# Two RMS norms by products with ones, other pieces of the first weights, and another order of the sample's values in a hybrid decoder step

## The chip, the cores and the metric

The kernel runs on one core of one Trainium2 chip. The time is the device time of one execution in microseconds (us), as a median over several runs. The engines are named as in the profile: PE is the matrix engine (TensorE), DVE the vector engine, ACT the scalar engine, POOL is GpSimd, SP issues most of the DMAs. Each engine works through its own written list of instructions strictly in order and waits for others only by semaphores.

## The reference

One step of one decoder layer, in fp32, for a prompt of 512 positions and 8 sample tokens, so that 520 columns share all weights. In short:

```python
h = rmsnorm(x, norm_mix_g)
q, k, v, u, xq, gates = split_cols(h @ w_in)
o_a = sliding_window_attention(q, k, v)            # 8 heads of 64, 2 kv heads, window 128, blocks of 128
o_b = s5_branch(u)                                 # scan, gelu, two products (glu)
mk, mv = split(rmsnorm(mem, norm_mem_g) @ w_mem_kv)
o_c = memory_attention(xq, mk, mv)                 # 4 heads of 128, 256 memory tokens
g = sigmoid(gates)
x += (g_A * (o_a @ w_br_attn) + g_B * o_b + g_C * (o_c @ w_br_mem)) @ w_out
x += (gelu(causal_conv3(rmsnorm(x) @ w_gate)) * (rmsnorm(x) @ w_up)) @ w_down
y = rmsnorm(x, norm_final_g)
```

The 8 sample tokens bring their own caches: the memory keys and values of the sample (`sk0` to `sk7`, `sv0` to `sv7` below) are read in units like weights.

## The kernel before

**Products.** x stands transposed, 1024 features in 8 blocks of 128 rows (`KB` = 8, "k blocks"), 520 columns in two halves of 260. Every fp32 number is split into a high part (fp32r) and the rest, and each product is made of three (`mm3`): high by high, high by rest, rest by high. A weight unit is 128 columns of a weight matrix, as 128 by 1024 numbers (512 KB). SP loads it into one of two raw buffers (`w_load`, tile `wraw`), ACT copies out the high part (`whi`), DVE subtracts to get the rest (`wlo`), and PE then runs 8 k blocks by 2 halves by 3 products, 48 matmuls. The units of the memory (`mv0` to `mk3`, over 256 tokens) take 24.

**Order.** Units run as written in `SEQ0` and `SEQ` (lines 51 and 53): first k and v together (the "kv" stage, `for k in range(KB)`, line 757), q0 to q3, then `u`, `mv`, `mk`, `xq`, then gates and the branch projections (`gA0 sk0 ...`, `PA`, `sv`, `gC`, `PC`), then glu, the output projection and the channel sub-layer, which the change leaves alone but for the last norm.

**Lanes.** The work beside the units (attention, norms, the S5 scan) is written as generators, "lanes", that yield between steps. While a kernel is written out, a planner (`Clock`, `pump`, `drain`) keeps an estimated clock for each engine and takes, between two products, the first lane that it holds to be ready. The schedule is manual: the order it arrives at is fixed in every engine's list, and the chip follows it whatever the real times are. `drain(lanes)` writes the lanes named to their end, with no products between.

**Sliding-window attention** (`swa`, line 879; 8 calls, two lanes of them running side by side) is a chain through three engines: 4 score products (PE), 4 maxima over scores and biases (DVE), negation, 4 exponentials (ACT), reciprocal and scaling (two heads on DVE, two on ACT), 8 transposes (PE), copies out of PSUM (DVE and ACT), products with v (PE), and the split of the result (ACT, then DVE). All calls must be through before `merged` is allotted: `drain(list(swa_lanes))` in line 1373, which stands between the units xq3 and gA0.

**The two norms.** The mixer norm sums x*x on DVE into `acc`; within q0, `rstd_cols` (line 570) sums over the partitions by 6 products of 88 columns by one, computes the reciprocal root by an integer guess and three Newton rounds on 88 by 6 numbers (11 small DVE instructions and one of 88 by 528), and `rstd_rows` spreads it over 128 rows by 6 products of 88 by 88 and ACT copies. `Q_COL` and `Q_ROW` say behind which blocks of q0 the two stand. The memory's norm (`mem_prep`, line 804) does the same for 256 tokens. k, v and q are multiplied by rstd when they are evacuated; from `u` on the units use a normalised x, which the lane `x_norm` (line 836) makes.

All instructions go through one wrapper in line 259, so that the profile shows L259 for nearly all of them; tiles are told apart by their names: `B` large buffers, `T` (T2) temporaries, `SD` PSUM of the lanes, `mm` PSUM of the units, `TN` tiny tiles.

## Time and profile before

| what | value |
|---|---|
| median of 3 runs | 869.65 us (869.54 to 870.18) |
| the profiled execution | 870.38 us, its span 868.6 us, mean granted clock 0.997 |
| PE busy | 851.2 us, 98% of the span |
| DVE, ACT, POOL busy | 599.8, 409.0, 135.7 us |
| bytes moved by DMA | 110.41 MB, 127 GB/s over the span |

The span is what the profile covers, from the first to the last instruction; 1.8 us of the profiled execution lie outside it. Busy time is the union of an engine's instructions. A timeline row may hold several records of one kind (x8), and a matmul in fp32 leaves two records. Matmuls are pipelined: one of 260 columns lasts 0.28 us in its record, but in a row of them one starts every 0.12 us. Idle time before an instruction is shown in brackets with what ended it.

### The profile page before, as it was taken

The page shows a single profiled execution, that of the slowest core. Times are in us where ns is not written, and L with a number is a line of the kernel's source. Part 1 is how long each engine was busy: PE and PEld are TensorE (multiplying, and loading weights), DVE is VectorE, ACT ScalarE, POOL GpSimd, SP SyncE. Part 2 cuts the span into 40 slices and gives each one's busy share as a digit, 9 for nine tenths or more (in the row PEclk, how much of TensorE's full clock was granted, in tenths as well). Part 3 has the DMA queues.
Part 4 walks back from the last instruction along what each step waited for, and adds up shares of the span by engine and source line. Part 5 has one row for each costly group of instructions (what it writes and reads, how often), then busy time and mean ns, then how long its engine had stood idle before and what let it go on. Part 6 is the DMA issues. An engine that isn't in the chain of part 4 may idle for free.

```text
span 868.6 us, 17715 instructions
## 1 busy us (share of the span) xinstructions
PE 851.2 (98%) x7067; PEld 823.0 (95%) x7067; DVE 599.8 (69%) x1101; ACT 409.0 (47%) x800; POOL 135.7 (16%) x370
## 2 busy tenths in 40 slices
PE   8999999999999999999999999999999999999996
PEld 8998899999789899989999999999999999999995
DVE  6786787985447698213765568787777877777756
ACT  7366565544434322223334434444645545464555
POOL 7888030000000000000000010111112110110100
PEclk9999999999999999999999999999999999999998
DMA  7534482253714523624333323557565655653222
GB/s 264 178 78 122 125 196 80 74 154 116 150 49 146 170 74 97 148 69 184 106 101 97 98 73 100 144 155 185 152 160 151 165 130 153 161 150 83 71 74 98
DMA packets 54737, 110.41 MB, mean 127 GB/s; under 512 B 13968, under 2 KB 25664, under 8 KB 54384
## 3 DMA queue, kind: packets, MB, share of 16 engines
q1 hardware_dynamic: 50816, 97.40, 38.0%
q0 software_dynamic: 3408, 11.27, 6.8%
q8 instruction: 55, 0.90, 0.4%
q10 hardware_dynamic: 432, 0.63, 0.2%
q14 instruction: 26, 0.21, 0.1%
HBM read 104.05 MB, written 6.26 MB: 127 GB/s over the span
## 4 chain that ended last, share of the span: by engine, by line
PE 74%; DVE 11%; issue 9%; ACT 3%; DMA 2%; SPq 0%; POOL 0%; DVEq 0%; ACTq 0%; POOLq 0%
PE mm L259 55%; PE SD L259 19%; DVE T L259 5%; DVE B L259 3%; DVE wlo L259 2%; DMA wraw<-in_w 2%; ACT T L259 1%; ACT whi L259 1%; ACT B L259 1%; DVE TN L259 1%; SPq L259 0%; POOL T L259 0%; DVE M L259 0%; DVEq L2334 0%; DVE it L259 0%
## 5 line engine op out<-in xcount | busy, mean ns | idle before, releaser
L259 PE MATMUL mm<-B,whi 128*128 128x260 f32 (+1 forms) x3632 | 666.5, 284 | 3.5 <-DVE B L259 1.4
L259 PEld LDWEIGHTS mm<-B,whi 128*128 128x128 f32 x3632 | 560.3, 188 | 11.9 <-issue 5.0
L259 PE MATMUL mm<-B,wlo 128*128 128x260 f32 (+1 forms) x1816 | 512.8, 282 | 1.9 <-DVE wlo L259 1.9
L259 PEld LDWEIGHTS mm<-B,wlo 128*128 128x128 f32 x1816 | 342.2, 188 | 2.8 <-DVE wlo L259 2.8
L259 DVE TENSOR_TENSOR wlo<-wraw,whi 128x1024 fp32r<-128x1024 f32 (+1 forms) x149 | 152.4, 1029 | 89.2 <-ACT whi L259 86.2
L259 ACT ACTIVATE whi<-wraw 128x1024 fp32r<-128x1024 f32 (+1 forms) x149 | 132.5, 897 | 73.0 <-PE mm L259 32.6
L259 PE MATMUL SD<-B,whi 128*128 128x260 f32 x464 | 85.9, 282 | 0.0
L259 PEld LDWEIGHTS SD<-B,whi 128*128 128x128 f32 x464 | 71.6, 188 | 0.1
L259 ACT ACTIVATE T<-mm 128x260 f32<-128x260 f32 (+3 forms) x76 | 32.5, 449 | 78.1 <-PE mm L259 78.0
L259 PE MATMUL SD<-B,wlo 128*128 128x260 f32 x232 | 65.6, 283 | 0.0
L259 ACT ACTIVATE B<-T 128x520 fp32r<-128x520 f32 (+2 forms) x48 | 29.7, 618 | 55.5 <-DVE T L259 55.4
L259 ACT ACTIVATE whi<-M 128x512 fp32r<-128x512 f32 x64 | 39.1, 624 | 26.3 <-DVE M L259 19.4
L259 DVE TENSOR_TENSOR wlo<-M,whi 128x512 fp32r<-128x512 f32 x64 | 42.8, 686 | 11.9 <-ACT whi L259 11.8
L259 DVE TENSOR_TENSOR B<-B 128x256 f32<-128x256 f32 (+11 forms) x78 | 36.3, 474 | 15.9 <-ACT B L259 14.4
L259 PEld LDWEIGHTS SD<-B,wlo 128*128 128x128 f32 x232 | 43.6, 188 | 0.0
L259 DVE TENSOR_TENSOR B<-mm,B 128x520 f32<-128x520 f32 (+2 forms) x36 | 22.4, 622 | 27.4 <-PE mm L259 26.8
L259 ACT ACTIVATE B<-SD 128x256 fp32r<-128x256 f32 (+5 forms) x44 | 17.9, 429 | 44.3 <-PE SD L259 44.3
L259 DVE TENSOR_TENSOR B<-SD,B 128x256 fp32r<-128x256 f32 (+6 forms) x43 | 16.5, 396 | 30.3 <-PE SD L259 22.7
L259 PE MATMUL SD<-B 128*64 128x72 f32 (+9 forms) x412 | 37.3, 282 | 0.0
L259 DVE SCALAR_TENSOR_TENSOR T<-T,sm,T 128x512 f32<-128x512 f32 x44 | 33.1, 753 | 2.7 <-ACT T L259 2.2
L259 DVE TENSOR_TENSOR B<-T,B 128x520 fp32r<-128x520 f32 (+2 forms) x50 | 31.2, 637 | 3.7 <-ACT B L259 3.4
L259 PEld LDWEIGHTS SD<-B 128*64 128x64 f32 (+4 forms) x412 | 25.6, 146 | 8.3 <-issue 4.0
(161 smaller groups left out, 801.8 us busy)
## 6 DMA issues: line engine op xcount, KB each, us to landing
wraw<-in_w SPq DMA_DIRECT2D x96, 512.0 KB, 3.6
M<-in_w SPq DMA_DIRECT2D x48, 256.0 KB, 3.6
wraw<-in_w SPq DMA_DIRECT2D x36, 256.0 KB, 3.3
T<-in_w SPq DMA_DIRECT2D x36, 192.0 KB, 4.4
M<-in_w POOLq DMA_DIRECT2D x8, 512.0 KB, 6.6
wraw<-in_w POOLq DMA_DIRECT2D x8, 512.0 KB, 6.3
sv<-in_w SPq DMA_DIRECT2D x12, 192.0 KB, 5.5
B<-in_xT SPq DMA_DIRECT2D x1, 2080.0 KB
```

The lines of the kernel that those rows point to most:

```text
L259: return g(*a, **k)
```

## The change

It has five parts. (1) Both norms sum over the partitions by products of a 128 by 128 matrix of ones with the sums of squares, so that every partition gets the sum; ACT then takes Ln and Exp for a first value and one Newton round of three DVE instructions runs on the full width. The table set for Ln and Exp is loaded at the start. (2) The first two weight units come in pieces of 1, 3 and 4 k blocks instead of two halves, and the loads of x stand between them. (3) Behind the mixer norm, `ahead` moves behind the evacuation of k and v, with the next weight split and one load in its old place. (4) In `SEQ` each `sv` unit moves behind a later unit, and PC0 to PC3 stand otherwise between the last gates. (5) In the last norm the square of the first value is taken by ACT instead of DVE.

```diff
-SEQ = 'gA0 sk0 gA1 sk1 gA2 sk2 gA3 sk3 gA4 sk4 gA5 sk5 gA6 sk6 gA7 sk7 PA0 PA1 sv0 PA2 sv1 PA3 sv2 gC0 sv3 gC1 sv4 gC2 sv5 sv6 gC3 sv7 gC4 PC0 gC5 PC1 gC6 gC7 PC2 PC3'
+SEQ = 'gA0 sk0 gA1 sk1 gA2 sk2 gA3 sk3 gA4 sk4 gA5 sk5 gA6 sk6 gA7 sk7 PA0 PA1 PA2 sv0 PA3 sv1 gC0 sv2 gC1 sv3 gC2 sv4 gC3 sv5 gC4 sv6 sv7 gC5 PC0 PC1 gC6 PC2 gC7 PC3'
...
-    act.activation(warm, ones[:, 0:1], AF.Exp)
+
+    nc.scalar.preload_act_table_set("natural_log_exp_and_others")
+    act.activation(warm, ones[:, 0:1], AF.Ln)
...
+    CUTS = (0, 1, 4, 8)
+    l0, l1 = w_load(0, CUTS), w_load(1, CUTS)
     next(l0)
     next(l1)
-    for k in (1, 2, 3):
-        x_load(k, 1)
+    x_load(0, 1)
+    x_load(1, 1)
+    next(l0)
+    next(l1)
+    x_load(2, 1)
+    x_load(3, 1)
     next(l0)
     next(l1)
...
+    def rstd_sums(part, out, n=NH, halves=(0, 1)):
+        pr = [SD() for _ in halves]
+        for p, h in zip(pr, halves):
+            pe.matmul(p[:, :n], ones, part[:, h * n:(h + 1) * n], start=True, stop=True)
+        for p, h in zip(pr, halves):
+            act.activation(out[:, h * n:(h + 1) * n], p[:, :n], AF.Ln, bias=eps, scale=1.0 / DM)
+        o = out[:, 0:len(halves) * n]
+        act.activation(o, o, AF.Exp, scale=-0.5)
+        v = T2(len(halves) * n)
+        for p, h in zip(pr, halves):
+            act.activation(v[:, h * n:(h + 1) * n], p[:, :n], AF.Identity, bias=eps, scale=1.0 / DM)
+            free(p)
+        return v, o
+
+    def newton(v, o):
+        t = T2(o.shape[1])
+        dve.tensor_tensor(t, o, o, op=OP.mult)
+        dve.scalar_tensor_tensor(t, t, -0.5, v, op0=OP.mult, op1=OP.mult)
+        dve.scalar_tensor_tensor(o, t, 1.5, o, op0=OP.add, op1=OP.mult)
+        free(t, v)
...
     for k in range(KB):
+        if k == 0:
+            for i in (ik, ik + 1):
+                w_split(i, 0, 1)
         split_norm(xraw, C_GMIX, xgh, xgl, k)
-        if k in (0, 2):
-            w_split(ik, k // 2)
-            w_split(ik + 1, k // 2)
-        if k:
+        if k in (1, 3):
+            for i in (ik, ik + 1):
+                w_split(i, CUTS[(k + 1) // 2], CUTS[(k + 3) // 2])
+        if k and k != 3:
             square(k - 1)
+        if k == 4:
+            square(2)
...
             if (h, k) == Q_COL:
-                dcol = rstd_cols([acc], (0, 1), NH)
-                ahead(iq)
-            if (h, k) == Q_ROW:
-                rstd_rows(dcol, rstd)
+                newton(*rstd_sums(acc, rstd))
+                w_split(iq + 1)
+                load(iq + 3)
...
     evac_kv(psv, vT, vs)
+    ahead(iq)
...
-        d = rstd_cols([macc], (0,), 256)
+        v, o = rstd_sums(macc, mrstd, 256, (0,))
         free(macc)
-        yield
-        rstd_rows(d, mrstd, 256, (0,))
-        free(d)
+        yield "dve", 1
+        newton(v, o)
         yield
...
             act.activation(self.v, self.pr, AF.Identity, bias=eps, scale=1.0 / DM)
+            self.t = T2(self.n)
+            act.activation(self.t, self.y, AF.Square)
 
         def newton(self):
-            t = T2(self.n)
-            dve.tensor_tensor(t, self.y, self.y, op=OP.mult)
+            t = self.t
```

Left out are the new signatures of `w_load` and `w_split`, which take k blocks to cut at.

The planner's lists change with it, from the start up to glu0. Three places follow; numbers behind a name tell one buffer from another.

PE of the kernel before, from the last products of unit mv0 (`mm_1222`): scores of one block of the sliding-window attention (`SD_1290`, `SD_1291`) and products with v of another (`SD_1308`).

```order
L259 MATMUL mm_1222<-B_593,whi_1039 128x256 x2
L259 MATMUL mm_1222<-B_593,wlo_1040 128x256
L259 MATMUL SD_1290<-B_123,B_594 128x256 [waits PE_49]
L259 MATMUL SD_1291<-B_123,B_594 128x256 [waits Activation_49]
L259 MATMUL SD_1290<-B_123,B_594 128x256
L259 MATMUL SD_1291<-B_123,B_594 128x256
L259 MATMUL SD_1308<-T2_1251,B_123 64x256 [waits DVE_49]
L259 MATMUL SD_1308<-T2_1252,B_123 64x256
L259 MATMUL SD_1308<-T2_1251,B_123 64x256
L259 MATMUL SD_1308<-T2_1252,B_123 64x256
```

PE of the changed kernel at the same place, between the units mv0 (`mm_1218`) and mv1 (`mm_1250`).

```order
L259 MATMUL mm_1218<-B_579,wlo_1011 128x256
L259 MATMUL mm_1218<-B_579,whi_1010 128x256 x2
L259 MATMUL mm_1218<-B_579,wlo_1011 128x256
L259 MATMUL mm_1250<-B_579,whi_1101 128x256 [waits PE_49,Activation_49]
L259 MATMUL mm_1250<-B_579,whi_1101 128x256
L259 MATMUL mm_1250<-B_579,wlo_1102 128x256
```

Unit mv1 follows at once. From mv0 to mk1 the changed kernel has six memory units with nothing between their products, and the attention's steps stand later.

PE of the kernel before at the seam between xq3 (`mm_2070`) and gA0 (`mm_2149`).

```order
L259 MATMUL mm_2070<-B_597,whi_1879 128x260
L259 MATMUL mm_2070<-B_598,whi_1879 128x260
L259 MATMUL mm_2070<-B_597,wlo_1880 128x260
L259 MATMUL mm_2149<-B_597,whi_1953 128x260 [waits Activation_49]
L259 MATMUL mm_2149<-B_598,whi_1953 128x260
```

PE of the changed kernel at the same seam, from the last product of xq3 (`mm_1859`) on. `SD_1995`, `SD_1996` are transposes of one attention block, called X below, `SD_2022` its products with v; `SD_2028`, `SD_2029` are transposes of a second, Y.

```order
L259 MATMUL mm_1859<-B_583,wlo_1709 128x260
L259 MATMUL SD_1995<-cs_123,T2_1773 128x128 [waits DVE_49,Activation_49]
L259 MATMUL SD_1995<-cs_123,T2_1773 128x128 x3
L259 MATMUL SD_1996<-cs_123,T2_1774 128x128 [waits DVE_49]
L259 MATMUL SD_1996<-cs_123,T2_1774 128x128 x3
L259 MATMUL SD_2011<-cs_123,B_126 8x128 [waits DVE_49]
L259 MATMUL SD_2011<-cs_123,B_126 8x128
L259 MATMUL SD_2022<-T2_2005,B_126 64x256 [waits DVE_49]
L259 MATMUL SD_2022<-T2_2006,B_126 64x256 [waits Activation_49]
L259 MATMUL SD_2022<-T2_2005,B_126 64x256
L259 MATMUL SD_2022<-T2_2006,B_126 64x256
L259 MATMUL SD_2028<-cs_123,T2_1904 128x128 [waits DVE_49,PE_49]
```

PE of the changed kernel, further on in the same seam: the scores of a third block, Z, the last of the eight (`SD_2043`, `SD_2044`), Y's products with v (`SD_2061`), and Z's transposes (`SD_2082`, `SD_2083`).

```order
L259 MATMUL SD_2043<-B_126,B_580 128x256 [waits PE_49]
L259 MATMUL SD_2044<-B_126,B_580 128x256 [waits DVE_49]
L259 MATMUL SD_2043<-B_126,B_580 128x256
L259 MATMUL SD_2044<-B_126,B_580 128x256
L259 MATMUL SD_2061<-T2_2038,B_126 64x256 [waits Activation_49]
L259 MATMUL SD_2061<-T2_2039,B_126 64x256
L259 MATMUL SD_2061<-T2_2038,B_126 64x256
L259 MATMUL SD_2061<-T2_2039,B_126 64x256
L259 MATMUL SD_2082<-cs_123,T2_2052 128x128 [waits DVE_49,Activation_49]
L259 MATMUL SD_2082<-cs_123,T2_2052 128x128 [waits Activation_49]
L259 MATMUL SD_2082<-cs_123,T2_2052 128x128 x2
L259 MATMUL SD_2083<-cs_123,T2_2053 128x128 [waits Activation_49] x2
```

Behind these stand Z's products with v (`SD_2099`), and then gA0. So 32 rows of attention lie between xq3's last and gA0's first product, where the kernel before has none.

ACT of the kernel before around the evacuation of xq3 (`M_1726<-mm_2070`).

```order
L259 ACTIVATE M_1726<-mm_1932 128x520 [waits PE_49]
L259 ACTIVATE whi_2083<-wraw_1957 128x1024 [waits DMAHW4_49]
L259 ACTIVATE M_1726<-mm_2070 128x520 [waits PE_49]
L259 ACTIVATE B_2135<-T2_2136 128x512 [waits DMASW2_49,Pool_49]
L259 ACTIVATE B_2135<-M_1726 128x16 [waits Activation_49]
L259 ACTIVATE B_2135<-T2_2136 128x512
```

ACT of the changed kernel from the evacuation of xq3 (`M_1504<-mm_1859`) on: the exponentials of Y (`T2_1904`, `T2_1905`), the copy of X's transposes (`T2_2006`), the scaling and copy of Y, the exponentials of Z (`T2_2052`).

```order
L259 ACTIVATE M_1504<-mm_1859 128x520 [waits PE_49]
L259 ACTIVATE T2_1904,TN_1903<-T2_1904,TN_1902 128x257 x2
L259 ACTIVATE T2_1905,TN_1903<-T2_1905,TN_1902 128x257 x2
L259 ACTIVATE T2_2006<-SD_1996 128x512 [waits PE_49]
L259 ACTIVATE T2_2014<-SD_2011 8x256 [waits PE_49]
L259 ACTIVATE T2_1905<-T2_1905,TN_1903 128x256 [waits DVE_49]
L259 ACTIVATE T2_1905<-T2_1905,TN_1903 128x256 [waits Activation_49]
L259 ACTIVATE B_793<-SD_2022 128x2x128 [waits PE_49]
L259 ACTIVATE T2_2039<-SD_2029 128x512 [waits PE_49]
L259 ACTIVATE B_793<-SD_2061 128x2x128 [waits PE_49]
L259 ACTIVATE T2_2052,TN_2051<-T2_2052,TN_2050 128x257 [waits DVE_49]
```

In the kernel before no step of the attention follows xq3's evacuation; in the changed one Y's exponentials and all of Z's stand behind it.

## Rows read from the trace of the kernel before

**Rows 1.** The page, busy time and share of the span of each engine
```profile
PE 851.2 (98%) x7067; PEld 823.0 (95%) x7067; DVE 599.8 (69%) x1101; ACT 409.0 (47%) x800; POOL 135.7 (16%) x370
```

**Rows 2.** The page, chain that ended last, shares by engine
```profile
PE 74%; DVE 11%; issue 9%; ACT 3%; DMA 2%; SPq 0%; POOL 0%; DVEq 0%; ACTq 0%; POOLq 0%
```

**Rows 3.** PE's timeline: start us, duration us, instruction, records; [idle before, what ended it]
```profile
1.05 4.64 PE L259 MATMUL SD<-ones 128*128 128x128 f32 x20 [1.05 <-DVE eps L259]
...
8.91 0.39 PE L259 MATMUL mm<-B,whi 128*128 128x260 f32 x1 [0.41 <-DVE B L259]
...
13.09 0.39 PE L259 MATMUL mm<-B,whi 128*128 128x260 f32 x1 [0.50 <-DVE B L259]
...
50.53 0.39 PE L259 MATMUL mm<-B,whi 128*128 128x260 f32 x1 [0.19 <-DVE B L259]
...
75.13 0.87 PE L259 MATMUL SD<-T,ones 88*128 88x88 f32 x6 [1.17 <-DVE TN L259]
...
233.94 2.00 PE L259 MATMUL SD<-T,M 128*128 128x256 f32 x8 [1.12 <-ACT T L259]
```

**Rows 4.** The chain of waits in the first 24 us: start, length, what
```profile
3.54 6.17 DMA wraw<-in_w
...
13.09 7.33 PE mm L259 x59
```

**Rows 5.** PE's timeline, products with ones
```profile
20.61 1.03 PE L259 MATMUL SD<-ones,T 128*88 128x1 f32 x12
...
25.18 1.47 PE L259 MATMUL SD<-T,ones 88*128 88x88 f32 x12
...
850.43 1.04 PE L259 MATMUL SD<-T,ones 128*128 128x260 f32 x4
```

**Rows 6.** ACT's timeline, steps of attention and an evacuation
```profile
71.02 0.51 ACT L259 ACTIVATE T<-T,TN 128x257 f32<-128x257 f32 x1 [1.68 <-DVE TN L259]
...
72.52 0.50 ACT L259 ACTIVATE T<-T,TN 128x257 f32<-128x257 f32 x1
...
75.10 0.91 ACT L259 ACTIVATE T<-T,TN 128x256 f32<-128x256 f32 x2 [2.00 <-DVE TN L259]
...
117.92 0.58 ACT L259 ACTIVATE T<-SD 128x512 f32<-128x512 f32 x1
...
148.49 0.60 ACT L259 ACTIVATE M<-mm 128x520 f32<-128x520 f32 x1 [4.19 <-PE mm L259]
```

**Rows 7.** DVE's timeline, steps of attention, x_norm's first step, one of the end
```profile
29.25 0.75 DVE L259 SCALAR_TENSOR_TENSOR T<-B,sm,rstd 128x520 f32<-128x520 f32 x1
...
69.01 0.47 DVE L259 CUSTOM_DVE_ANT_0 T<-SD,B,sm 128x256 f32<-128x256 f32 x1
...
75.10 0.69 DVE L259 TENSOR_TENSOR T<-T,TN 128x512 f32<-128x512 f32 x1
...
860.77 0.29 DVE L259 TENSOR_TENSOR T<-T 128x130 f32<-128x130 f32 x1 [0.33 <-ACT T L259]
```

**Rows 8.** PE's timeline, one attention block's products
```profile
66.72 1.13 PE L259 MATMUL SD<-B 64*128 64x256 f32 x8
...
77.70 1.03 PE L259 MATMUL SD<-cs,T 128*128 128x128 f32 x8
...
140.35 1.08 PE L259 MATMUL SD<-T,B 128*64 128x256 f32 x8
```

**Rows 9.** The page, loads of the weights: KB each, us to landing
```profile
wraw<-in_w SPq DMA_DIRECT2D x96, 512.0 KB, 3.6
```

**Rows 10.** Windows of the end: busy us (count) per engine, granted clock, DMA
```profile
core 0: us, PE busy (x) PEld busy (x) DVE busy (x) ACT busy (x) POOL busy (x), PEclk, DMA share, GB/s
...
860.00:862.50 2.50, 0.15 (x2) 0.00 (x0) 2.00 (x6) 2.31 (x8) 0.00 (x0) 1.00 0.56 213
...
862.75:868.00 5.25, 0.00 (x0) 0.00 (x0) 2.50 (x6) 0.00 (x0) 0.00 (x0) 0.50 0.53 203
```

**Rows 11.** ACT's timeline, a load of function tables
```profile
236.37 1.28 ACT L259 ACT_TABLE_LOAD   x1
```

More of the change, by code (lines that the diff above doesn't have):

```diff
@@ L359, in body, with w_load, w_split @@
     RAW, HI, LO = {}, {}, {}
-    def w_load(i, parts=1):
+    def w_load(i, cuts=None):
         if i >= len(UNITS) or i in RAW:
             return
-        n = unit_blocks(UNITS[i]) * P
+        n = unit_blocks(UNITS[i])
         r = clk.tile(wrw.tile([P, KB * P], F32, name="wraw", tag="wraw"), "wraw", N_RAW)
         RAW[i] = r
-        m = n // parts
-        for c in range(parts):
-            yield sp.dma_start(r[:, c * m:(c + 1) * m],
-                               bass.AP(tensor=I["w"].tensor, offset=I["w"].offset + UNIT_OFF[i] + c * m,
-                                       ap=[[n, P], [1, m]]))
-    def w_split(i, part=None):
-        if i >= len(UNITS) or (part is None and i in HI):
+        cuts = cuts or (0, n)
+        for a, b in zip(cuts, cuts[1:]):
+            yield sp.dma_start(r[:, a * P:b * P], bass.AP(tensor=I["w"].tensor, offset=I["w"].offset + UNIT_OFF[i] + a * P,
+                                                          ap=[[n * P, P], [1, (b - a) * P]]))
+    def w_split(i, a=0, b=None):
+        if i >= len(UNITS) or (b is None and i in HI):
             return
@@ L378, in w_split @@
             pass
-        n = unit_blocks(UNITS[i]) * P
-        if not part:
+        if a == 0:
             HI[i] = clk.tile(wsp.tile([P, KB * P], F32R, name="whi", tag="whi"), "whi", 3)
             LO[i] = clk.tile(wsp.tile([P, KB * P], F32R, name="wlo", tag="wlo"), "wlo", 3)
-        c = slice(0, n) if part is None else slice(part * n // 2, (part + 1) * n // 2)
+        c = slice(a * P, (b or unit_blocks(UNITS[i])) * P)
         r = RAW[i]
@@ L535, in x_load @@
         sp.dma_start(xraw[:, k * NT:(k + n) * NT], I["xT"][:, k * NT:(k + n) * NT])
-    l0, l1 = w_load(0, 2), w_load(1, 2)
-    x_load(0, 1)
+    CUTS = (0, 1, 4, 8)
+    l0, l1 = w_load(0, CUTS), w_load(1, CUTS)
     next(l0)
     next(l1)
-    for k in (1, 2, 3):
-        x_load(k, 1)
+    x_load(0, 1)
[4 more added lines that the diff above has]
+    x_load(3, 1)
     next(l0)
@@ L760, in body @@
                 mm3(ps[:, h, :NH], wh, wl, xh, xl, k == 0, k == KB - 1)
-    w_split(ik + 2, 0)
+    w_split(ik + 2, 0, 4)
     square(KB - 1)
-    w_split(ik + 2, 1)
+    w_split(ik + 2, 4, 8)
     load(ik + 3)
```

## The prediction

> **What bounds the kernel now.** I read the busy times first, then the chain of waits, then PE's timeline for its idle time, then the timelines of the engines that it waits for. The busy times show one full engine: PE works for 851.2 of 868.6 us [rows 1]. The chain that ends last runs on PE for 74%, on DVE for 11% [rows 2]. So a part of the change counts if it shortens PE's own list, or opens or closes a gap in it; time saved on DVE or ACT alone counts for nothing. PE's timeline has few gaps where the change works: the start, where the hot matmuls run to 5.4 us and k and v then wait several times (0.41 and 0.50 us are two of those waits); 0.19 us in u0; 1.17 us in the memory's norm; 1.12 us in PA1 [rows 3].
>
> Beside the gaps the order counts. In each engine's list the instructions run as written, so a chain of attention costs PE nothing while products stand between its steps, and its whole latency where none do. The changed order takes them away at one place, and that term decides my sum.
>
> **The change, part by part.** The sum is made against the profiled execution (870.38 us, span 868.6). That is 0.7 us over the median of 869.65, to which I add the same differences.
>
> *Pieces of the first weights.* Products start at 5.40 us, when the hot matmuls end. Products follow each other at 0.124 us (59 in 7.33 us [rows 4]), and of the 96 of k and v these 59 begin at 13.09, so the first 37 took 7.7 us where 4.6 would do: 3.1 us is all there is to win. The kernel before waits until 9.71 for the second halves [rows 4]. In the changed kernel the last pieces stand behind the same 2,088 KB (four blocks of x at 266 KB, 1,024 KB of weights), so I put their landing at 9.7 too. They bring blocks 4 to 7 only, so blocks 1 to 3 come sooner. What follows is DVE's list: two subtractions of wlo, then x's fifth block, then two sums of squares that were put off, then the sixth block. With ACT's two copies of 0.6 and DVE's steps of 0.65 each, the sixth block is there at about 14.4, and three blocks of 12 products are 4.5 us more: an end near 18.9. With one more wait like those of now [rows 3] I take 19.2 in place of 20.26: **−1.05** (bounds −0.3, if x's blocks are late behind the pieces, and −3.1).
>
> *Mixer norm.* In q0, 12 records of 88 by 1 and 12 of 88 by 88 go. They start 0.073 and 0.105 us apart (1.03 and 1.47 us with the pipelined ends [rows 5]), 2.14 us in all. Two products of ones by 260 columns come; in the last norm two such took 1.04 us as four records [rows 5], 0.43 each without the shared end. Net **−1.27** (−1.0 to −1.5).
>
> *What u0 gives back.* u0 needs the normalised x, and waits for DVE at its end already [rows 3]. x_norm's first step stands at 29.25 [rows 7]. In the changed order there stand before it three Newton steps of 0.67, two wlo, and the evacuations of k, v and q0; from the norm's sums at 20.4, Ln and Exp to 21.8, I get 28.3 for it, so 0.9 to 1.1 us earlier, and not the 2.3 that PE is ahead. The steps behind it are partly paced by the q units, which come 2.3 earlier. I take 1.7 in all: **+0.6** (0 to +1.3).
>
> *Memory's norm.* The wait of 1.17 at 75.13 [rows 3] has DVE's small steps behind it. They go; so do 6 records of 88 by 1 and 6 of 88 by 88 (1.07 us by the spacings above), for one product of 0.43. Together **−1.8** (−1.1, if the new product waits half as long, to −2.0). It stands behind DVE's last sum of squares within u3, and products with v within xq2 come one product behind what they wait for. For these I put two waits of the size of 0.41 and 0.50 [rows 3], **+0.9** (0 to 2). The six bare memory units ask for 512 KB every 24 products, 2.9 us; a load takes 3.6 [rows 9], and with its copy and subtraction, over two buffers, about as long as the products. I put nothing (0 to +0.9).
>
> *The seam between xq3 and gA0.* The changed order has 32 rows of attention there, and none of them products of units. Three blocks (X, Y, Z) are unfinished, and Y and Z have their exponentials behind xq3's evacuation in ACT's list, which must wait for xq3's last product. From that product, t = 0:
>
> ACT evacuates, 0.60, to 0.7; four exponentials of Y take from 71.02 to 73.1 in the trace, 2.1, to 2.8; the copy of X's transposes 0.58, to 3.4 [rows 6]. Only then PE goes on with X's products with v (it has done X's transposes meanwhile), to 4.3; Y's transposes, 1.0, to 5.3; Z's scores, of which the second half waits for X's last step on DVE (5.95), end at 6.8; Y's products with v at 7.8 [rows 8]. Z's maxima, negation and start of the exponentials take 2.0 (69.01 on DVE to 71.02 on ACT [rows 6, 7]): 8.8. Exponentials, 2.1: 10.9. Reciprocal and scaling, 0.17 and 0.91 on ACT beside 0.69 on DVE [rows 6, 7]: 12.0. PE, idle from 7.8 to 11.9, transposes until 12.8; copies to 13.5; products with v, 1.08 with their pipelined end, until 14.4. There gA0 begins. PE's own work in it is three transpositions of 1.0, three products with v of 1.0, scores 1.1 and 0.25 of small ones, 7.3 us, which the kernel before does elsewhere. So PE stands **+7.1**. The lower bound: were Y's exponentials done before xq3 ends, Z's chain alone remains: its scores at 4.2, the end at 10.9, so 3.6. The upper: DVE or ACT late by the two scan steps and wlo that stand in between, some 2 us, 9.1.
>
> *Order of `sv` and PC.* At PA1 PE waits 1.12 for ACT [rows 3], which waits for DVE behind a wlo of 1.2; in the changed order that wlo stands behind: **−1.0** (−1.1 to 0). The other places keep a pair of `sv` units (now ahead of gC5), with the same wait. *Last norm.* One DVE step of 0.29 [rows 7] goes to ACT, which comes to it earlier: **−0.3** (−0.6 to +0.1).
>
> *Tables.* A further table load stands ahead of gA0's gates, as the set of the start has no tanh; a load takes 1.28 [rows 11] on ACT. In gA0 PE has products of its own, so nothing (0 to +1.3). On the price, the Trainium skill ("ScalarE: Activation LUTs", What ACT_TABLE_LOAD costs) adds a drain to the load and has 2.66 us per switch. By it the upper end would be 1.4 higher; the row has 1.28, and no row here shows the drain.
>
> Sum: −1.05 −1.27 +0.6 −1.8 +0.9 +7.1 −1.0 −0.3 = +3.2, so 873.6 against the profiled execution and **872.8** against the median.
>
> **The rivals.**
>
> *The clock falls in the seam.* At the end of the kernel PE's last product ends near 860.15; the granted clock is 1.00 until 862.5 and 0.50 from 862.75 on [rows 10]. So it fell from 2.4 to 1.2 GHz while PE stood still, and in the seam PE stands still for 4.1 us before Z's transposes. At the start the hot matmuls took 4.35 us for 20 records, 0.217 each [rows 3], where products take 0.124; a stretch like that at half speed, Z's last 2 us and gA0's first, loses 2.2. Then 875.0 (874 to 877). Against it: three shorter gaps and little work lie around it, and the end of the kernel is one case. The Trainium skill says the same of idle time ("TensorE: Matmul & The Clock Gate", HAM oscillation): waits between bursts of products let the clock fall back, and the next burst starts at half. By that rule this rival holds; the trace agrees at its end.
>
> *Not slower: the gains come whole and the seam is short.* If x's pieces cover k and v fully (−3.1), u0 gives nothing back and no new small wait comes, the others add to −7.5 and the seam's 7.1 leaves 869.3, no change. With the seam's lower bound of 3.6 it is 865.8. The place that decides is ACT at the seam: if Y's exponentials run while xq3's products still do, Z's chain starts some 3.5 us sooner. For it speaks that ACT is busy less than half of the time [rows 1]; against it that they stand behind an evacuation that waits for PE.
>
> *The change is neutral in the seam*: PE comes late to xq3's end, held by DVE, so that the attention has caught up. Then the loss stands in xq0 to xq3 in place of the seam, about as large, and the time is that of the forecast.
>
> **How the numbers follow.** The forecast with its terms' bounds, 870.8 to 874.8, holds 0.53 of the chance (with the third rival in it), the fallen clock 0.20, the second rival 0.27: no change within it 0.16 and faster 0.11. What a measurement tells from no change is 0.2%, 1.7 us: 867.9 to 871.4. The forecast's own range dips into it for 0.08 (a further 0.02 below). So slower 0.63, same 0.24, faster 0.13. The range of 867.5 to 877 leaves out the second rival's gains and a clock that falls twice.
>
> **What would show it.** In the changed profile, PE should have two long gaps between xq3's last product and gA0's first, about 2 us before X's products with v and about 4 before Z's transposes, both ended by ACT or DVE; gA0 should start 14 us behind xq3's end. The 1.17 of the memory's norm should be gone, and k and v should end near 19.2. A granted clock under 1 behind the seam shows the first rival. The prediction is wrong if PE idles under 4 us in the seam, or if u0 starts more than 3 us earlier than now.

## The result and the profile after

The changed kernel takes 882.6 us (median of 4 runs, 881.27 to 883.8), the kernel before 869.62 beside it: a ratio of 1.0147 [1.0133, 1.0161], 13.0 us slower. The forecast was 872.8, with a range of 867.5 to 877. The sign of the forecast was right, its size was not. The profiled execution took 882.45 us with a span of 880.7, 12.1 more than the span of before, and that is the difference followed here.

The page of the changed kernel, its busy times and its chain by engine, which answer to [rows 1, 2]:

```profile
PE 854.3 (97%) x7037; PEld 824.5 (94%) x7037; DVE 595.5 (68%) x1080; ACT 413.3 (47%) x811; POOL 139.9 (16%) x370
...
PE 70%; DVE 13%; issue 9%; ACT 5%; DMA 1%; POOL 0%; SPq 0%; DVEq 0%; ACTq 0%; POOLq 0%
```

PE has 30 records fewer and yet is busy 3.1 us longer: some of its products ran at a lower clock. Its idle time is 26.4 us where it was 17.4. PE's timeline of the changed kernel shows where; its rows answer to [rows 3, 5, 8].

```profile
6.28 0.39 PE L259 MATMUL mm<-B,whi 128*128 128x260 f32 x1 [1.38 <-ACT B L259]
...
20.09 0.40 PE L259 MATMUL SD<-B,whi 128*128 128x260 f32 x2
...
69.87 0.70 PE L259 MATMUL SD<-T,ones 128*128 128x256 f32 x2
...
80.43 0.51 PE L259 MATMUL mm<-B,whi 128*128 128x256 f32 x2 [2.46 <-ACT T L259]
...
88.35 0.47 PE L259 MATMUL mm<-B,whi 128*128 128x256 f32 x2 [1.90 <-DVE B L259]
...
96.33 0.47 PE L259 MATMUL mm<-B,whi 128*128 128x256 f32 x2 [0.51 <-DVE B L259]
...
145.71 0.65 PE L259 MATMUL SD<-T,B 128*64 128x256 f32 x2 [0.38 <-DVE T L259]
147.37 1.08 PE L259 MATMUL SD<-T,B 128*64 128x256 f32 x6 [1.02 <-ACT T L259]
148.38 1.09 PE L259 MATMUL SD<-cs,T 128*128 128x128 f32 x8
...
150.88 1.08 PE L259 MATMUL SD<-T,B 128*64 128x256 f32 x8
155.75 1.94 PE L259 MATMUL SD<-cs,T 128*128 128x128 f32 x8 [3.79 <-DVE T L259]
157.62 2.72 PE L259 MATMUL SD<-T,B 128*64 128x256 f32 x8
160.28 0.79 PE L259 MATMUL mm<-B,whi 128*128 128x260 f32 x2
...
161.39 2.75 PE L259 MATMUL SD<-M 128*128 128x256 f32 x12
...
862.89 1.04 PE L259 MATMUL SD<-T,ones 128*128 128x260 f32 x4
```

The memory's norm (69.87) has lost its wait of 1.17. The seam is there: X's products with v at 145.71 and 147.37, Y's transposes at 148.38 and its products at 150.88, then 3.79 us of nothing, Z's transposes and gA0. But there are three waits that the prediction did not have, 2.46, 1.90 and 0.51, each ahead of the products of a memory unit (256 columns). And Z's transposes and products take 1.94 and 2.72, where Y's, the same instructions 7 us earlier, take 1.09 and 1.08. The windows of the changed kernel say why (busy us and count of PE, PEld, DVE, ACT and POOL, then the granted clock, the DMA share, GB/s):

```profile
8.00:10.00 2.00, 2.00 (x11) 2.00 (x11) 1.69 (x4) 2.00 (x5) 1.66 (x5) 0.50 1.04 379
...
74.00:100.00 26.00, 21.14 (x160) 20.59 (x160) 10.81 (x25) 10.20 (x23) 12.85 (x46) 0.93 0.50 143
...
90.00:92.00 2.00, 2.00 (x11) 2.00 (x11) 0.00 (x0) 0.00 (x0) 0.00 (x0) 0.50 1.02 307
...
140.00:168.00 28.00, 22.82 (x146) 18.12 (x145) 16.59 (x53) 18.21 (x53) 1.59 (x3) 0.88 0.06 20
152.00:154.00 2.00, 0.00 (x0) 0.00 (x0) 1.54 (x7) 1.79 (x7) 0.00 (x0) 1.00 0.00 0
154.00:156.00 2.00, 0.25 (x2) 0.28 (x3) 1.27 (x4) 1.58 (x6) 0.00 (x0) 0.53 0.00 0
156.00:158.00 2.00, 2.00 (x9) 1.58 (x9) 1.83 (x5) 0.27 (x1) 0.00 (x0) 0.50 0.00 0
```

and, of the kernel before, the window of the start and the same two long ones:

```profile
8.00:10.00 2.00, 1.59 (x13) 1.39 (x13) 1.51 (x2) 1.48 (x4) 1.70 (x4) 1.00 1.05 378
...
74.00:100.00 26.00, 24.87 (x201) 21.94 (x201) 18.61 (x55) 17.58 (x58) 10.69 (x41) 1.00 0.39 118
140.00:168.00 28.00, 28.00 (x257) 26.10 (x256) 22.91 (x58) 15.63 (x38) 1.82 (x5) 1.00 0.23 71
```

A clock of 0.50 is 1.2 GHz, 1.00 is 2.4. It fell in three places: at the start, in the memory units, and in the seam. In the kernel before it stays at 1.00 in all three.

Why the memory units wait stands in the timelines of three other engines. ACT of the changed kernel, at u3's evacuation (`T<-mm`, 256 columns) and at the copies of the weights for the memory units:

```profile
76.56 1.31 ACT L259 ACTIVATE T<-T,TN 128x256 f32<-128x256 f32 x3 [1.71 <-DVE TN L259]
...
79.35 1.02 ACT L259 ACTIVATE T<-mm 128x256 f32<-128x256 f32 x3
...
85.55 1.06 ACT L259 ACTIVATE whi<-wraw 128x1024 fp32r<-128x1024 f32 x1 [4.31 <-DMA wraw<-in_w]
87.01 1.06 ACT L259 ACTIVATE whi<-wraw 128x1024 fp32r<-128x1024 f32 x1 [0.40 <-DMA wraw<-in_w]
93.53 1.06 ACT L259 ACTIVATE whi<-wraw 128x1024 fp32r<-128x1024 f32 x1 [5.47 <-DMA wraw<-in_w]
```

and SP's queue, which issues the stores of u (`ud`, `us`) and the loads of the weights (`wraw`) in the order of its list:

```profile
67.46 0.45 SPq L259 DMA_DIRECT2D wraw<-in_w  x1
80.39 0.37 SPq L259 DMA_DIRECT2D ud<-T  x1
...
81.48 23.36 SPq L259 DMA_DIRECT2D wraw<-in_w  x8
```

and DVE, the second part of a weight block (`wlo`) and the evacuation of a memory unit (`B<-mm,B`):

```profile
86.64 1.23 DVE L259 TENSOR_TENSOR wlo<-wraw,whi 128x1024 fp32r<-128x1024 f32 x1 [3.81 <-ACT whi L259]
87.79 0.42 DVE L259 TENSOR_TENSOR B<-mm,B 128x256 f32<-128x256 f32 x1
```

Read from the end backwards: PE waits at 88.35 for the evacuation that DVE begins at 87.79. That stands behind the `wlo` of 86.64, this behind ACT's copy of 85.55, and the copy waited 4.31 for a block that landed only then. The block was issued at 81.48, since SP stood at u3's stores from 67.9 to 80.39. The stores waited for u3's evacuation at 79.35, which stands on ACT behind one block's scalings and the next block's four exponentials (from 76.56 on), and these waited 1.71 for DVE. The first memory unit's products, behind u3's, were done at 78.0; then PE itself waits 2.46 for the same evacuation, without any load between. For 13.6 us no weight was asked for. The row of 81.48 merges eight loads; the second is issued at 82.53, the third at 87.90.

The difference from before, at marks that both traces have (start of a PE row or of an evacuation; the forecast is the sum of the prediction's terms up to there, with the 7.3 us of attention taken out of the stretch ahead of the seam):

| mark | before | after | measured | forecast |
|---|---|---|---|---|
| q0's first product | 20.26 | 20.09 | -0.2 | -1.05 |
| u0's evacuation | 54.01 | 52.84 | -1.2 | -1.7 |
| xq3's evacuation | 148.49 | 144.28 | -4.2 | -9.9 |
| gA0, the row `SD<-M` x12 | 149.01 | 161.39 | +12.4 | +4.5 |
| last norm's product with ones | 850.43 | 862.89 | +12.5 | +3.5 |
| span | 868.6 | 880.7 | +12.1 | +3.2 |

Of the miss of 8.9 us, 5.2 arise between u0 and xq3, 2.2 in the seam, 1.0 behind it, and about half a microsecond ahead of u0. Behind the seam PE has a wait of 0.92 at 201.74 and one of 0.75 at 209.46, both for a `wlo` of DVE, where the kernel before has one of 0.81 at 178.29; what brings the second is open (e3 and e10 are without it).

### The profile page after: what moved, and what is told of

Same layout as the page of the kernel before. It is cut to its first block, busy times and chain, and to the rows that moved or that the text cites. A ratio compares the mean times of both kernels' runs of the same rounds, so it can differ in the third digit from the quotient of the medians.

```text
span 880.7 us, 17645 instructions
## 1 busy us (share of the span) xinstructions
PE 854.3 (97%) x7037; PEld 824.5 (94%) x7037; DVE 595.5 (68%) x1080; ACT 413.3 (47%) x811; POOL 139.9 (16%) x370
## 4 chain that ended last, share of the span: by engine, by line
PE 70%; DVE 13%; issue 9%; ACT 5%; DMA 1%; POOL 0%; SPq 0%; DVEq 0%; ACTq 0%; POOLq 0%
PE mm L259 52%; PE SD L259 18%; DVE T L259 5%; DVE B L259 4%; DVE wlo L259 3%; ACT T L259 3%; ACT whi L259 2%; DMA wraw<-in_w 1%; ACT B L259 1%; DMA B<-in_xT 0%; POOL T L259 0%; DVE TN L259 0%; ACT rstd L259 0%; DVE M L259 0%; SPq L259 0%
## 5 line engine op out<-in xcount | busy, mean ns | idle before, releaser
L259 DVE TENSOR_TENSOR wlo<-wraw,whi 128x1024 fp32r<-128x1024 f32 (+3 forms) x151 | 153.0, 1020 | 116.1 <-ACT whi L259 115.4
L259 ACT ACTIVATE whi<-wraw 128x1024 fp32r<-128x1024 f32 (+3 forms) x151 | 132.3, 888 | 73.6 <-PE mm L259 29.8
L259 POOL MEMSET T<- 128x2 f32 (+2 forms) x27 | 7.7, 285 | 207.7 <-PE SD L259 111.3
```

What stands on the lines that cost most here:

```text
L259: return g(*a, **k)
```

## The experiments

All ratios are against the kernel before on the same chip. Differences from the changed kernel are of medians on different chips, where the kernel before took 869.6 to 870.0 us, so they hold to about 0.4 us. Of the expectations, those of e4, e9 and e11 missed; e1, e2, e5 and e8 came out 0.04 to 0.2 us above the range of the theory that they bear out, and e3 and e13 0.5 and 0.2 below it; e2 kept a wait of 2.33 that its theory excludes.

**e1, the memory's norm as before, all else changed.**
```diff
-        v, o = rstd_sums(macc, mrstd, 256, (0,))
+        d = rstd_cols([macc], (0,), 256)
...
-        yield "dve", 1
-        newton(v, o)
+        yield
+        rstd_rows(d, mrstd, 256, (0,))
+        free(d)
```


> The changed kernel with the memory's norm alone written as before (sums by 88 columns, small DVE steps, rows spread by products); all other parts stay. Theory O (the time is lost by the places of the attention's steps in the lists: with this norm the planner again puts them between the memory units, and the seam between xq3 and gA0 is empty): the changed kernel's 2.46, 1.90 and 0.51 us of waits in the memory units, the low clock there (1.7), and some 9 us of the seam go, and the norm's own wait of 1.2 and 0.6 of products come back: 868 to 871 us. Theory P (the new steps cost by themselves, Ln and Exp and full-width rounds on ACT and DVE, and more table loads, wherever they stand): only the memory norm's share changes, 880 to 884 us.

871.04 us, 1.0015 [1.0002, 1.0028]: 11.5 us less than the changed kernel. The seam is empty (PE busy for all of 140 to 168). Its PE timeline has one wait instead, where the norm's old small steps stand:

```profile
75.67 1.55 PE L259 MATMUL SD<-T,ones 88*128 88x88 f32 x6 [2.46 <-DVE T L259]
```

The profiled execution of e1 is the slowest of its nine (874.58; the fastest took 869.4): behind this one wait the clock is at 0.50 from 76 to 82. So the seam and the late loads both hang on the memory's norm, but the norm alone does not say how: e4.

**e2, the lists' rule loosened.** The planner takes a step of the attention behind a product only while its own reckoning of DVE and ACT stands within a limit of PE (`pump`); in the memory units the limit is raised by 3 us.
```diff
-    def pump(rem=0.0):
+    def pump(rem=0.0, slack=0.0):
...
-            if clk.t["dve"] - t > min(BACK_D, lim) or clk.t["act"] - t > min(BACK_A, lim):
+            if clk.t["dve"] - t > min(BACK_D, lim) + slack or clk.t["act"] - t > min(BACK_A, lim) + slack:
...
-                pump(1.3)
+                pump(1.3, 3)
...
-        pump()
+        pump(0.0, 3)
```


> The changed kernel with all of its parts; only the planner's limit on how far DVE and ACT may be ahead of PE is 3 us wider within the memory units, so that attention's steps stand between them again, and none in the seam. Theory O: 867 to 870 us, no wait over 1 us in the memory units and no seam. Theory P: nothing of the new steps is taken out, so 880 to 884 us. A third way: the steps are back between the units, but PE now waits for DVE and ACT there instead, 872 to 878 us.

870.05, 1.0006 [0.9996, 1.0015]: 12.5 us less than the changed kernel. With attention between the memory units' products again the seam is gone (140 to 168 full, clock 1.00). The loads still go out late, at 81.28, and waits of 2.33 (at 80.22, for u3's evacuation) and 0.84 (at 90.32) stay, with a clock of 0.91 in 80 to 100. So the seam is made of what the memory units did not take. The waits behind the late loads are 0.84 where the changed kernel has 1.90 and 0.51; the one for the evacuation itself is as long as there.

**e3, products of ones in the seam.** The lists are those of the changed kernel, but for 12 products in PE's longest gap, ahead of Z's transposes.
```diff
+        if (b, ip) == (3, 1):
+            for _ in range(12):
+                nc.tensor.matmul(pp[0][:, 0:P], ones, ones, start=True, stop=True)
```


> The changed kernel with every list as it is, and 12 products of ones (128 by 128, 0.24 us each at the high clock) put on PE in front of Z's transposes in the seam, into a bank that these overwrite. If the clock fell because PE stood still for 3.8 us there, it stays at 1.00: Z's transposes take 1.0 instead of 1.9, its products with v and gA0's first go at full pace, and 2.5 to 3.2 us are won: 879.4 to 880.1 us. If the clock falls for another reason, or the products push the transposes back, 882 to 884 us.

878.89, 1.0106 [1.0091, 1.0121]: 3.7 us less than the changed kernel; the only edit is work that does nothing. Its PE timeline, gA0's first products last, and the window that had 0.50:

```profile
151.33 2.94 PE L950 MATMUL SD<-ones 128*128 128x128 f32 x24
155.19 1.06 PE L259 MATMUL SD<-cs,T 128*128 128x128 f32 x8 [0.91 <-DVE T L259]
156.83 1.19 PE L259 MATMUL SD<-T,B 128*64 128x256 f32 x8 [0.57 <-DVE T L259]
157.95 0.51 PE L259 MATMUL mm<-B,whi 128*128 128x260 f32 x2
```
```profile
156.00:158.00 2.00, 1.43 (x12) 0.81 (x10) 1.87 (x5) 0.60 (x1) 0.00 (x0) 1.00 0.00 0
```

Z's rows are back at 1.06 and 1.19, 2.4 us less than 1.94 and 2.72, and 0.57 of it goes into a new wait for DVE. From xq3's evacuation to the row `SD<-M` x12 the two traces differ by 2.1 us (15.05 against 17.11). So the first rival's mechanism is shown, and its price, forecast as 2.2. The rest of the 3.7 lies elsewhere in the two executions: 0.6 ahead of the seam (e3's kept the clock at 1.00 at the start) and 0.9 behind it, where e3 lacks the wait of 0.75.

**e4, the memory's norm and the table load alone,** on the kernel before (e1's lines in the other direction, cut here).
```diff
+    nc.scalar.preload_act_table_set("natural_log_exp_and_others")
...
+        v, o = rstd_sums(macc, mrstd, 256, (0,))
```

> The kernel before with the memory's norm alone in its new form (and the table set preloaded). Theory O: the planner puts attention's last steps into the seam here too (it does, three lanes are open there), and the memory units stand bare: slower than before by 6 to 13 us, 876 to 883 us. Theory P: the new norm saves its wait of 1.2 and 0.6 of products: 867.5 to 870 us.

871.06, 1.0012 [1.0002, 1.0022], where theory O expected 876 or more: a miss. The 1.17 is gone, the memory units do not wait, and a seam of two blocks (waits of 0.30, 1.10, 0.34) takes the gain back. The norm opens a small seam by itself; the large one and the late loads need another part too.

**e5, all parts but the move of `ahead`.**
```diff
-                w_split(iq + 1)
-                load(iq + 3)
+                ahead(iq)
...
-    ahead(iq)
```


> The changed kernel with `ahead` back in its place right behind the mixer norm; both new norms, the pieces and the order of the units stay. Theory M (the move of `ahead` sends the weight splits and loads of the u units later, so that u3's evacuation and the stores behind it hold up SP's loads and PE stands 2.4 us in the memory units; with it in its old place that wait and the low clock behind it go, and the seam holds two blocks as in the kernel before with the memory norm alone): 869 to 872 us. Rival: the move costs nothing and the memory norm alone makes bare units and seam: 880 to 883 us.

872.19, 1.0023 [1.0014, 1.0033]: 10.4 us less than the changed kernel. The loads are on time, the seam has two blocks, the clock holds. PE's timeline of it, q1's first product and the seam:

```profile
28.03 0.48 PE L259 MATMUL mm<-B,whi 128*128 128x260 f32 x2 [1.20 <-DVE B L259]
...
144.84 1.08 PE L259 MATMUL SD<-T,B 128*64 128x256 f32 x6 [1.15 <-ACT T L259]
...
147.29 1.42 PE L259 MATMUL SD<-T,B 128*64 128x256 f32 x8 [0.35 <-DVE T L259]
```

Further on it has a wait of 2.03 for ACT (224.12), near the place of PA1's 1.12 in the kernel before. The move takes a wait of 1.20 from q1, and the whole order behind it comes out otherwise. In e5's list ACT evacuates u3 at 74.31, ahead of the second block's exponentials, and in the changed kernel behind them. PE's own time does not decide it on the chip: it reaches the first memory unit at 74.78 in e5 and at 74.94 in the changed kernel. Which of the planner's clocks turns the order round is not shown.

**e6, the pieces of the first weights alone.**
```diff
-    CUTS = (0, 4, 8)
+    CUTS = (0, 1, 4, 8)
```
(with the loads of x between them as in the change)

> The kernel before with the first weights in pieces of 1, 3 and 4 k blocks (part 2) alone. By my prediction k and v end 1.05 us earlier and half of it is given back at u0: 868.8 to 869.6 us beside 870.0 of before on this chip. By the trace of the changed kernel (products start 0.9 us later, as x's first block stands behind two weight pieces, and the clock falls at the gap behind the hot products): no change, 869.5 to 870.5 us.

869.44, 0.9995 [0.9987, 1.0004]: nothing. The norm's products start at 20.56 instead of 20.61.

**e7, the mixer norm alone,** with `ahead` at its old place.
```diff
-                dcol = rstd_cols([acc], (0, 1), NH)
+                newton(*rstd_sums(acc, rstd))
                 ahead(iq)
-            if (h, k) == Q_ROW:
-                rstd_rows(dcol, rstd)
```
(the table load of the start is the new one, as in e4)

> The kernel before with the mixer norm alone in its new form, `ahead` in its old place. By my terms: 1.27 us of products go in q0 and some 0.6 come back at u0, 869.0 to 869.6 us beside 870.0. Rival: u0 waits for DVE, whose new full-width steps are as long as the old small ones, and gives all of it back: 869.8 to 870.4 us. If the planner's other order behind it holds new waits in u3 and the memory units: 871 us or more.

870.09, 1.0003 [0.9994, 1.0012]: nothing. At q1's first product PE waits 1.21 for DVE (at 29.98), which takes back the 1.27 of the small products: from q0's first product to u0's evacuation it takes 33.69 us, and the kernel before 33.75.

**e8, all parts with `ahead` at its old place, e2's limit, and x's first block loaded ahead of the weights.** Its diff is e5's and e2's, and
```diff
+    x_load(0, 1)
     next(l0)
     next(l1)
-    x_load(0, 1)
```

> All new operations of the change, but `ahead` in its old place, the planner's limit 3 us wider in the memory units, and x's first block loaded ahead of the first weight pieces. Theory O: no wait over 1 us in the memory units, no seam, products from 5.4 us on: the gains of my sum without its losses (1.0 at the start, 1.3 in q0 less 0.6, 1.8 in the memory norm, 0.3 at the end): 866 to 868 us. If the parts give nothing by themselves: 869.5 to 871 us.

868.13, 0.9985 [0.9976, 0.9994]: the first version below the kernel before. No wait in the memory units, no seam; q1's 1.22 remains.

**e9, u's stores issued by ACT,** so that the loads on SP stand behind no store; no other list changes.
```diff
-        sp.dma_start(ud[:, m].rearrange("j p t -> p j t"), uT[:, 0:512].rearrange("p (j t) -> p j t", j=8))
-        sp.dma_start(us[m], uT[:, 512:NT])
...
+            nc.scalar.dma_start(o_, i_)
```


> The changed kernel with every list as it is, but the eight stores of the u units (ud, us) issued by ACT behind its evacuation and not by SP. If the loads of the memory units are late because SP's queue stands at u3's store until u3 is evacuated, the next load is issued some 7 us sooner than 81.5, the waits of 1.9 and 0.5 us in the memory units and the low clock behind them (1.7) go, and the 2.46 (which waits for the evacuation itself) stays: 878 to 880 us beside 882.6. If the loads are late for another reason (raw buffers, or the time a load takes), 882 to 883 us.

885.84, 1.0182 [1.0168, 1.0196]: 3.2 us worse. The load that stood at 81.48 now goes out at 73.29, and the wait of 1.90 for DVE at the memory units went. But the next load goes out only at 87.50, when ACT's copy, still behind u3's evacuation, has freed a raw buffer; ACT now stands at each pair of stores, and PE waits for ACT. SP's, ACT's and PE's timelines of e9:

```profile
73.29 0.33 SPq L259 DMA_DIRECT2D wraw<-in_w  x1
...
87.50 0.33 SPq L259 DMA_DIRECT2D wraw<-in_w  x1
```

```profile
68.36 0.59 ACTq L1336 DMA_DIRECT2D us<-T  x1
69.00 0.51 ACT L259 ACTIVATE B<-M,sm 128x256 fp32r<-128x256 f32 x1 [1.08 <-issue]
```
```profile
70.90 0.80 PE L259 MATMUL SD<-T,B 128*64 128x256 f32 x4 [2.87 <-ACT T L259]
...
84.14 0.51 PE L259 MATMUL mm<-B,whi 128*128 128x256 f32 x2 [1.87 <-ACT T L259]
```

That the stores held the first of the loads is shown by its issue 8.2 us sooner and by the wait that went; that freeing them in this way helps is refuted. The 1.87 at 84.14 is the changed kernel's 2.46, the wait for u3's evacuation itself.

**e10, six more hot products at the start,** to close the gap ahead of 6.28.
```diff
+    for _ in range(6):
+        nc.tensor.matmul(hot[:, 0:P], ones, ones, start=True, stop=True)
```


> The changed kernel with every list as it is, and 6 more products of ones behind the 10 at the start, so that PE does not stand still before x's first block is there. If the low clock in k and v (7 to 11 us) comes from that gap, it stays at 1.00 and up to 1.7 us are won, less in runs that kept it anyway: 881 to 882.3 us. If it does not: 882.3 to 883 us.

882.25, 1.0137 [1.0121, 1.0152]: as the changed kernel. The clock is 1.00 from 6 to 12 and the products follow at full pace, but then PE waits. Two rows of its timeline:

```profile
15.72 0.39 PE L259 MATMUL mm<-B,whi 128*128 128x260 f32 x1 [0.39 <-DVE B L259]
...
20.41 0.60 PE L259 MATMUL SD<-T,ones 128*128 128x260 f32 x2
```

The norm's products start at 20.41 against 20.44. In e10 the start is set by DVE's work on x's sixth block, begun at 14.91; the changed kernel's begins at 14.74, so at full clock it could have been some 0.2 us sooner. The half clock there costs no more than that.

**e11, e3, e9 and e10 together.** Their diffs, added.

> The changed kernel with the stores of u on ACT, the 6 more products at the start and the 12 filling products in the seam, every list otherwise as it is. If the three causes are apart from each other, their gains add up: some 3.5 us in the memory units, 3.7 in the seam and 0.7 at the start, 874 to 875.5 us; what is left above 870 is then the seam's idle time and the one wait of 2.5. If they hide each other (the clock low either way, or the time is taken by the next wait), 877 us or more.

882.19, 1.0143 [1.0129, 1.0158]: the gains expected do not come, as e9 brought none. What the three gave alone (+3.2, -3.7 and -0.4) adds to -0.9, and -0.4 is measured, which the difference between chips covers. The seam's clock holds, and the waits that e9 brought (2.86 at 71.14, 1.88 at 85.71) take it back.

**e12, the order of `sv` and PC alone** (the change's line of `SEQ`, cut here, on the kernel before).
```diff
-... PA0 PA1 sv0 PA2 sv1 PA3 sv2 gC0 sv3 ...
+... PA0 PA1 PA2 sv0 PA3 sv1 gC0 sv2 gC1 ...
```

> The kernel before with part 4 alone: the new order of `sv` and PC in SEQ. My term: the wait of 1.12 at PA1 goes and nothing comes in its place, 868.6 to 869.2 us beside 869.65. Rival: the planner's lists put another wait of the same size behind it (the changed kernel has 0.92 and 0.75 at gA4 and gA5 that before has not), so no change, 869.4 to 870.2 us.

870.04, 1.0002 [0.9993, 1.0010]: nothing that the times can tell. The 1.12 at PA1 is gone, and waits of 0.26 (229.66) and 0.15 (321.40) are new. From gA0's row `SD<-M` x12 to the last norm the trace is 0.5 us shorter than that of before, half of the term; 0.5 lies within the interval of the times.

**e13, u3's evacuation ahead of the exponentials.** All parts of the change, e2's limit at 2 us, and no step of attention behind the last four k blocks of u3's second half.
```diff
-                        pump(0.325 * ((1 - h) * n + n - 1 - k))
+                        if not (UNITS[i][:2] == ("u", 3) and h == 1 and k >= 4):
+                            pump(0.325 * ((1 - h) * n + n - 1 - k))
...
-                pump(1.3)
+                pump(1.3, 2)
...
-        pump()
+        pump(0.0, 2)
```


> As e2 (all parts of the change, the planner's limit wider in the memory units, here by 2 us), but the planner starts no attention step within the last products of u3, so that ACT evacuates u3 before the four exponentials. If the evacuation's place is the cause, the wait of 2.3 us in the memory units, the 0.8 behind it and the low clock (1.8) of e2 go: 866 to 868 us beside 869.8 of before. If the loads come late all the same (raw buffers, or the load's own time), the units wait for weights and the time stays at 869 to 871 us.

**865.82, 0.9956 [0.9943, 0.9968]: 4.0 us faster than the kernel before, 16.8 faster than the changed one,** with all of its parts kept. ACT's timeline, SP's queue and the two long windows of e13:

```profile
74.02 1.11 ACT L259 ACTIVATE T<-mm 128x256 f32<-128x256 f32 x3 [1.71 <-PE mm L259]
74.94 0.52 ACT L259 ACTIVATE T<-T,TN 128x257 f32<-128x257 f32 x1
```
```profile
75.15 0.37 SPq L259 DMA_DIRECT2D ud<-T  x1
...
76.25 8.56 SPq L259 DMA_DIRECT2D wraw<-in_w  x3
```
```profile
74.00:100.00 26.00, 26.00 (x215) 24.26 (x215) 17.52 (x55) 18.93 (x64) 11.27 (x38) 1.00 0.48 137
140.00:168.00 28.00, 28.00 (x257) 26.01 (x257) 23.63 (x52) 16.02 (x37) 2.02 (x5) 1.00 0.26 77
```

The evacuation now stands ahead of the exponentials (74.02 instead of 79.35) and the loads go out 5.2 us sooner. PE stands still in neither stretch and the clock stays at 1.00. Attention runs in the memory units again (55 DVE and 64 ACT instructions in 74 to 100, where the changed kernel had 25 and 23), so none is left for a seam. Two edits work together here: the limit, which alone gave 870.05 (e2, at 3 us), and the place of u3's evacuation, which takes off 4.2 us more. That place alone, and e2's limit at 2 us, were not run.

**e14, e13 with x's first block loaded ahead of the weights** (e13's diff and e8's last).

> As e13, and x's first block loaded ahead of the first weight pieces, as e8 has it. By e8's trace products start at about 6.1 instead of 6.3 us and the clock holds at the start, so 0 to 0.5 us less than e13: 865.7 to 868 us. If the start's gap costs nothing in most runs (as e10 showed for the filled gap), the same as e13.

867.18, 0.9970 [0.9959, 0.9982]: 1.4 more than e13, with intervals that overlap. The norm's products start at 20.94 instead of 20.62. With x's first block ahead, the sixth block reaches PE at 16.17 (e8) and 16.27 (e14), without it at 15.44 to 15.96 (seven runs): the blocks that set the pace come later. Of the 1.0 us between the two traces 0.3 arises there and 0.7 behind gA0, among it a wait of 0.40 at 226.16; why is open.

## Why the prediction was right in sign and wrong in size

*The step that failed:* "The six bare memory units ask for 512 KB every 24 products ... I put nothing (0 to +0.9)". The stretch cost 6.3 us: 2.46 of waiting for u3's evacuation itself, for which the sum had no term; 2.41 (1.90, 0.51) behind late loads; and 1.5 at half clock (the 48 products from 88.35 to 95.82 took 7.5, the 48 from 80.43 to 86.45 took 6.0). The loads, two at a time, took up to 5.6 us (issued at 87.90, copied from 93.53) where the prediction had 3.6 [rows 9]; the larger error was the start of the loads. They were counted as if SP were free to issue them. In SP's list they stand behind u3's stores, those behind u3's evacuation, and that behind four exponentials on ACT. The prediction followed ACT's list at xq3 step by step, and not at u3, where the same pattern stands 65 us earlier: an evacuation and exponentials in one queue. e9 took away the stores, and the 1.90 went while the wait for the evacuation stayed (1.87). e13 put the evacuation ahead of the exponentials, with attention back between the units, and all three waits went.

*A step left out:* the move of `ahead` had no term of its own. e5 puts 10.4 of the 13.0 us on it, and e1 11.5 on the memory's norm; they are one cost that needs both. As the code reads, the planner holds DVE and ACT to be further behind PE in the memory units than its limit allows, so it takes no attention there, and the attention ends up in the seam. That the limit in `pump` decides is shown by e2, where raising it alone emptied the seam and took 12.5 us off; why these two parts together run into it, and neither alone, is not shown.

*The seam: right.* Forecast 14.4 us from xq3's end, with gaps of about 2 and 4; from xq3's evacuation to gA0 it is 16.0, with gaps of 0.38 + 1.02 and 3.79, ended by DVE and ACT. With the clock held it is 14.2 (143.72 to 157.95 in e3). PE stands still for 5.2 us of it, not 7.1: its own products fill more of it than the 7.3 put, in part at half clock.

*The clock, the first rival: it came too,* in the seam at the price given (e3), and at the memory units, where the prediction did not look. The price was read off the hot matmuls of the start as a stretch at half speed, but the profile of the kernel before gives 1.00 for them from 1 to 5.5 us, so that it came out so close is in part luck. The Trainium skill ("TensorE: Matmul & The Clock Gate", HAM oscillation) has waits between bursts of products let the clock fall back; the prediction held this at 0.20, with the trace's end as its one case, and the trace now agrees in the seam (0.50 behind 3.79 us).

*Start, -1.05: measured -0.2, and nothing in e6.* The prediction had "the sixth block is there at about 14.4". PE gets it at 15.7 (e10's row), and 35 products at 0.12 later it is 20.0. The later products ran at full pace as forecast; DVE's list took longer than reckoned.

*Mixer norm, -1.27, and u0, +0.6:* up to u0 the sum was -1.7 and measured -1.2. Alone the norm gains nothing (e7), since q1 then waits 1.21; only with `ahead` out of the way (no such wait in the changed kernel) does it count.

*Memory's norm, -1.8:* its wait is gone, as forecast. *The new small waits, +0.9:* none came. *Order of `sv` and PC, -1.0:* PA1's wait went; alone that is worth 0.5 in the trace (e12), and in the changed kernel the waits of 0.92 and 0.75 take it back (from gA0 to the last norm +0.1). *Last norm, -0.3:* from its product with ones to the span's end -0.4. *Tables, 0:* the load stands in gA0, and PE waits for nothing there.

*The second rival:* its 865.8 was to come from a short seam and full gains at the start. e13 comes to 865.82, but by chance: it is another kernel, without any seam. What its trace wins over that of before is 1.0 us from q0 to u0, 2.3 from u0 to xq3, 0.7 from gA0 to the last norm and 0.4 behind it, and nothing at the start: about the forecast's own gains (0.7, 1.8, 1.0 and 0.3), without what the lists took back.

## What to carry to other kernels

A planner that sets the order from its own clocks can turn a gain of about two microseconds ahead of a stage into a loss of ten behind it, so read the new order at every stage that the gain reaches, not only where the change is made. When a list has loads behind stores on one queue, follow the store back to the work that it waits for, and count the load from there; its own duration does not say when it lands. And where PE waits for a few microseconds, price what follows at half clock too: 12 products that do nothing were worth 2.1 us in the seam.

## What the runs showed of the hardware

- Behind one wait of PE of 2.46 us at the memory's norm (e1), or of 2.33 (e2), 2.45 (e3, e10) or 1.87 (e9) in the memory units, the granted clock fell to 0.50 for 3 us or more, in e1 for 6. In the changed kernel the wait of 2.46 left it at 1.00, and it fell behind the next, of 1.90. Waits of 1.88 (e11), 2.03 (e5), 1.17 and 1.12 [rows 3] left it at 1.00. So the changed kernel's list in the memory units lost its clock at one place in one execution (89 to 93 us) and at another in the next (e10, 81 to 84).
- A half clock can cost next to nothing: from 8 to 10 us the changed kernel ran at 0.50 and e10 at 1.00, and their norms start at 20.44 and 20.41, since PE would have waited for DVE.
- A pair of stores issued by ACT holds ACT's next instruction by 1.08 us (e9, at 69.00 and at 85.16), on an engine that was busy for under half of the span.
- Moving one load of x ahead of the weights made the sixth block reach PE later, at 16.17 and 16.27 (e8, e14) against 15.44 to 15.96. The first product came no sooner than in other executions (6.07 and 6.14 against 6.07 to 6.74).
